# A transformer layer's gate-up projection: the next group's first split moved behind two result additions, and five raw buffers shared by all pairs

## The chip, the cores and the metric

The kernel runs on one core of one Trainium2 chip. The metric is the device time of one execution in microseconds (us). Before the change the median of 3 runs is 1850.49 us (1850.45 to 1850.53). Engines are named as the profile names them: PE is TensorE (matmul), PEld its weight loads, DVE is VectorE, ACT is ScalarE, POOL is GpSimd, SP is SyncE, whose queue issues most DMAs.

## The reference

One encoder layer on 256 tokens of width 2048, all in float32: a feed-forward half step, a mixer (a gated linear recurrence beside windowed attention), and a second feed-forward half step. The change lies in the feed-forward part, which the program runs twice:

```python
def swiglu(x, w_gate_up, w_down):
    gate, up = jnp.split(x @ w_gate_up, 2, axis=-1)
    return (jax.nn.silu(gate) * up) @ w_down

ff = swiglu(rms_norm(x, pre_norm_ffn1[layer]), w_ffn1_gate_up[layer], w_ffn1_down[layer])
x = x + 0.5 * rms_norm(ff, post_norm_ffn1[layer])
```

`x` is 256 x 2048, `w_gate_up` is 2048 x 11264 (5632 gate columns, then 5632 up columns), `w_down` is 5632 x 2048.

## The kernel before, in words

**Products.** Each float32 operand is held as two parts: h, the value rounded to the format that the PE multiplies in, and l, the remainder. A product of two operands takes three matmuls (h by h, h by l, l by h; `three`, lines 435 to 448). ACT makes h with a cast and DVE makes l with a subtraction (`split_act`, lines 175 to 177; L176 is every cast and L177 every such subtraction of the program). `split_half` does this for half of a raw tile, 128 x 1024, in h and l tiles of which there are five each.

**Groups and pairs.** The gate-up product is made in 11 groups g of 512 gate and 512 up columns. A group goes through the 2048 rows of the weight in 8 pairs u, each of two blocks of 128 rows. A pair's raw weights are one tile of 128 x 2048 floats, loaded in two DMAs of 512 KB. The result of a group stands in four banks of PSUM, `c[m][n]` with m the half of the tokens and n gate or up; below they are called c(m,n).

**Plain and mixed pairs.** A plain pair makes 8 products (24 matmuls). A mixed pair makes 7 (21 matmuls, `products`, lines 485 to 509), by the scheme that multiplies 2 x 2 blocks with seven products: some go to four further banks, p1, p5, p6 and p7, which have to be added to the c banks at the end of the group, and the weights have to be summed before they are split. In groups 2 to 10 pairs 2, 4, 5 and 6 are mixed, in group 1 pairs 2 and 4, in group 0 none (`MIXED_IN`, line 847). A mixed pair is prepared first (`prepare`, lines 894 to 906): its first block is split, and a DMA issued by POOL then adds its second block to the first in the raw tile. Its other three halves are split later (`splits`, lines 908 to 927).

**Loads before the change.** `plan` (lines 876 to 885) makes two lists, of the mixed and of the plain pairs. Mixed pairs use the pool `rawp` with three buffers, plain pairs the pool `room` with two. When the last half of a pair has been split, `load_next` takes the next pair of the same kind from its list and issues its two DMAs on SP (line 152, in `load`).

**Order of work.** From group 1 on the order of the instructions on each engine is the order in which the program states them (`tc.manual_schedule`, line 1167): splits are stated one pair ahead of the products that use them (`first_pairs`, `pair_ahead`). An engine takes its instructions in that order; semaphores alone hold it back.

**The boundary** (`boundary`, lines 1101 to 1127) ends each of the groups 1 to 9, so there are nine in each of the two feed-forward layers. Pair 7, the last one, is plain, and its products are stated bank by bank, c(0,0), c(1,0), c(0,1), c(1,1), six matmuls each (`bank`). Before each bank's products the mixed pairs' part is added to it on DVE:

- ACT copies p1 to a (L1112); c(0,0) += a (L1113)
- b = p6 + a (L1116); a = p7 + b (L1117); c(1,0) += a (L1118)
- b = p5 - b (L1121), formed in place; c(0,1) += b (L1122)
- b = p5 - a (L1124), formed in place; c(1,1) += b (L1125)

Between the first and the second of these lines stands the first half of the split of the next group's pair 0 (a cast on ACT and a subtraction on DVE); its second half stands behind the last. Pair 6, just ahead of the boundary, is mixed and writes last into p7, p6 and c(1,0), in this order. Behind the boundary `units` (lines 1033 to 1080) applies silu and the product of gate and up, and transposes the result.

Of the kernel before, what the change touches and what calls it, by code (L numbers as in the profile page):

```python
# [11 lines left out]
F32 = mybir.dt.float32  # L12
# [8 lines left out]
P = 128  # L21
# [3 lines left out]
KT = D // P  # L25
# [12 lines left out]
def hymba_layer_kernel(  # L38
# [25 lines left out]
    nc = tc.nc  # L64
# [3 lines left out]
    rawp = ctx.enter_context(tc.tile_pool(name="rawp", bufs=3))  # L68
# [7 lines left out]
    def nm(s):  # L76
        uid[0] += 1
        return f"{s}_{uid[0]}"
# [62 lines left out]
    def load(src, between=None, pool=rawp, **kw):  # L141
        raw = pool.tile([P, 2048], F32, tag="raw", name=nm("raw"), **kw)
        if len(src.shape) == 4:

            dst = raw.rearrange("p (a n b) -> p a n b", a=src.shape[1], n=src.shape[2])
            parts = [(dst[:, a], src[:, a]) for a in range(src.shape[1])]
        else:
            parts = [(raw.rearrange("p (a b) -> p a b", a=src.shape[1]), src)]
        for i, (to, of) in enumerate(parts):
            if i and between:  # L150
                between()
            nc.sync.dma_start(to, of)
        return raw
# [14 lines left out]
    def split_half(raw, i, hp=hip, lp=lop):  # L168
        part = raw[:, i * 1024 : (i + 1) * 1024]
        h = hp.tile([P, 1024], F32R, tag="h", name=nm("h"))  # L170
        l = lp.tile([P, 1024], F32R, tag="l", name=nm("l"))
        split_act(h, l, part)
        return h, l
# [24 lines left out]
    def close_far():  # L198
        far["cm"].__exit__(None, None, None)
# [193 lines left out]
    def sums_of(u, w):  # L393

        nc.vector.tensor_tensor(
            w[:, S3::2, :], u[:, 0, :].rearrange("p (m t) -> p m t", m=2), u[:, :, P:T], ALU.subtract
        )
        nc.vector.tensor_tensor(w[:, S2, :], w[:, S1, :], u[:, 0, 0:P], ALU.subtract)
        nc.vector.tensor_tensor(w[:, S4, :], u[:, 1, 0:P], w[:, S2, :], ALU.add)
        return w  # L400

    class Blocks:
# [4 lines left out]
        ahead = None  # L407
# [437 lines left out]
    LATE = 8  # L845

    MIXED_IN = (2, 4, 5, 6)
    AWAY = 8
    MIXED = range(0, 20, 2)
    MIXED_EARLY = MIXED[:8]  # L850
# [4 lines left out]
    class Gated(Blocks):  # L855
# [20 lines left out]
        def plan(self):  # L876

            self.here = {g: MIXED_IN if g > 1 else MIXED_IN[:2] for g in range(1, NG)}
            self.kinds = {True: [], False: []}
            for g in range(1, NG):  # L880
                for u in range(KT // 2):
                    self.kinds[u in self.here[g]].append((g, u))
            self.raws, self.firsts, self.split_of = {}, {}, {}
            for mixed in (False, True, False, True, True):
                self.load_next(mixed)

        def load_next(self, mixed):

            if self.kinds[mixed]:
                g, u = self.kinds[mixed].pop(0)  # L890
                kw = {} if mixed else {"pool": self.room, "bufs": 2}
                self.raws[g, u] = load(self.source(u, g), **kw)

        def prepare(self, g, u):

# [12 lines left out]
        def splits(self, g, u):  # L908

            raw = self.raws[g, u]  # L910
            got = self.split_of[g, u] = []
            if (g, u) in self.firsts:
                b11, b12, b21, b22 = (raw[:, i * 512 : (i + 1) * 512] for i in range(4))
                got.append(split_half(raw, 1))
                nc.vector.tensor_tensor(b22, b11, b22, ALU.add)
                nc.vector.tensor_tensor(b21, b22, b21, ALU.add)
                yield
                got.append(split_half(raw, 0))
                yield
                got.append(split_half(raw, 1))  # L920
                self.load_next(True)
            else:
                got.append(split_half(raw, 0))
                yield
                got.append(split_half(raw, 1))
                self.load_next(False)
            yield

        def take(self, g, u):
# [41 lines left out]
    def ffn(gated, w_dn, post_gain, again, gain=None, lead=None, aside=None):  # L971

        with ExitStack() as st:
            work = st.enter_context(tc.tile_pool(name=nm("wk"), bufs=1, reuse_waits="tile"))
            late = st.enter_context(tc.tile_pool(name=nm("hl"), bufs=LATE, reuse_waits="tile"))
            early_cm = tc.tile_pool(name=nm("he"), bufs=NU - LATE - AWAY, reuse_waits="tile")
            early = early_cm.__enter__()
# [5 lines left out]
            def room_for(tag):  # L983
                return work.tile([P, 512], F32, tag=tag, name=nm(tag))
# [21 lines left out]
            def even(u):  # L1006

                x = gated.tiles[u].rearrange("p k i t -> p (k i) t")
                nc.vector.tensor_tensor(
                    x, x.bitcast(F32), R[:, None, :].to_broadcast([P, 4, T]), ALU.mult  # L1010
                )

            def sums_in(u):
                x = gated.tiles[u].bitcast(F32)
                whole = room_for("z").rearrange("p (k t) -> p k t", k=2)
                nc.vector.tensor_tensor(whole, x[:, :, 0, :], x[:, :, 1, :], ALU.add)
                ws = sums_of(whole, room_for("s").rearrange("p (j t) -> p j t", j=4))
                apart = u == MIXED_IN[1]
                w = (gated.room if apart else work).tile(
                    [P, 4, 2, P], F32R, tag="sp", name=nm("xs"), bufs=1 if apart else 3  # L1020
                )
                split_act(w[:, :, 0, :], w[:, :, 1, :], ws)
                gated.sums[u] = w

            def put_away(u):
                away[u] = dram.tile([P, 1024], F32, tag=f"ht{u}", name=nm("away"))
                nc.sync.dma_start(away[u], hts[u].bitcast(F32).rearrange("p k i t -> p (k i t)"))
# [5 lines left out]
            def units(c, scale):  # L1033
# [34 lines left out]
                for bank in banks:  # L1068
                    g = len(hts)
                    u = bank.rearrange("p (k t) -> p k t", k=2)  # L1070
                    if g in MIXED_EARLY:
                        u = room_for("z").rearrange("p (k t) -> p k t", k=2)
                        nc.scalar.copy(u.rearrange("p k t -> p (k t)"), bank)
                    pool = early if AWAY <= g < NU - LATE else late
                    ht = pool.tile([P, 2, 2, T], F32R, tag="ht", name=nm("ht"))
# [6 lines left out]
            def some(steps, n):  # L1082
                for _ in range(n):
                    next(steps)
# [3 lines left out]
            for u in range(gated.pos, KT // 2):  # L1088
# [4 lines left out]
                for done in {4: (0, 1, 2), 5: (3, 4), 6: (5, 6), 7: (7,)}.get(u, ()):  # L1093
                    even(done)
                    if done in MIXED_IN[:2]:
                        sums_in(done)
# [4 lines left out]
            def boundary(g):  # L1101

                a, b = room_for("z"), room_for("s")
                c, (p1, p5, p6, p7) = gated.c, gated.p
                add = nc.vector.tensor_tensor
                rest_of = gated.take(g, last)

                def bank(m, n):
                    for k in range(2):
                        rest_of[4 * k + 2 * m + n]()  # L1110

                nc.scalar.copy(a, p1)  # L1112
                add(c[0][0], c[0][0], a, ALU.add)  # L1113
                ahead = gated.splits(g + 1, 0)
                next(ahead)
                add(b, p6, a, ALU.add)  # L1116
                add(a, p7, b, ALU.add)  # L1117
                add(c[1][0], c[1][0], a, ALU.add)  # L1118
                bank(0, 0)
                bank(1, 0)  # L1120
                add(b, p5, b, ALU.subtract)  # L1121
                add(c[0][1], c[0][1], b, ALU.add)  # L1122
                bank(0, 1)
                add(b, p5, a, ALU.subtract)  # L1124
                add(c[1][1], c[1][1], b, ALU.add)  # L1125
                bank(1, 1)
                next(ahead)

            def first_pairs(g, waiting):

                gated.group(g)
                some(waiting, 1)
                gated.prepare(g, MIXED_IN[1])
                some(waiting, 1)
                ahead = gated.splits(g, 1)
                some(ahead, 2)
                gated.prepare(g, MIXED_IN[2])
                for one in gated.take(g, 0):
# [9 lines left out]
            def pair_ahead(g, u):  # L1148

                ahead = gated.splits(g, u + 1)  # L1150
                next(ahead)
                if u + 1 == MIXED_IN[1]:
                    gated.prepare(g, MIXED_IN[3])
# [5 lines left out]
                if g == 1 and u in (4, 5):  # L1159
                    sums_in(MIXED_IN[u - 2])  # L1160
                if u == 5 and 1 < g <= AWAY // 2 + 1:
                    put_away(2 * g - 4)
# [4 lines left out]
            with tc.manual_schedule():  # L1167
                gated.prepare(1, MIXED_IN[0])
                some(gated.splits(1, 0), 2)
                for g in range(1, NG):  # L1170
# [3 lines left out]
                    if g < NG - 1:  # L1174
                        ahead = gated.splits(g, last)
# [24 lines left out]
            close_far()  # L1200
            back_cm = tc.tile_pool(name=nm("hb"), bufs=AWAY, reuse_waits="tile")
            back = back_cm.__enter__()
# [27 lines left out]
    def two_banks():  # L1230
        return [[pa(), pa()], [pb(), pb()]]

    gated = Gated(w_ffn1_gate_up[0], two_banks())
    xt = new_xt()
    gated.see(xt)
    with tc.manual_schedule():
# [9 lines left out]
        raw = rawp.tile([P, 2048], F32, tag="raw", name=nm("raw"))  # L1246
# [121 lines left out]
    with ExitStack() as s2:  # L1368
# [367 lines left out]
        for hp in range(4):  # L1736
            zf = headpair(2048 + hp * 256, "zf")
            if hp == 1:
                g = gates(0)
# [18 lines left out]
        g = gates(1)  # L1758
# [13 lines left out]
        gated = Gated(w_ffn2_gate_up[0], two_banks())  # L1772
# [80 lines left out]
```

## Time and profile before

| what | value |
|---|---|
| median of 3 runs | 1850.49 us |
| the profiled execution | 1851.23 us |
| its span, first to last instruction | 1849.5 us |
| PE busy | 1816.7 us, 98% |
| DVE busy | 1628.2 us, 88% |
| ACT busy | 1127.2 us, 61% |
| DMA | 422.42 MB, mean 228 GB/s |
| granted PE clock | 0.999 |

The span is cut in the profile into groups of instructions by line; a group's row gives busy time, the mean length of one and the idle time of the engine just ahead of them with what ended it. The chain of waits gives 53% of the span to L441, the line of all matmuls of `three`. Matmuls are pipelined: a 128x512 matmul is shown with 0.39 us, while the starts of two that follow each other without a stop are 0.23 us apart.

### The profile page before, as it was taken

To read this page: it belongs to the slowest core of one execution; us is meant where nothing else is said; L and a number is where in the kernel's file an instruction comes from. 1 tells how busy PE (TensorE), PEld (TensorE's weight loads), DVE (VectorE), ACT (ScalarE), POOL (GpSimd) and SP (SyncE) were. 2 spreads that over 40 slices of the span, in tenths; PEclk is the share of its full clock that TensorE was granted. 3 is DMA by queue.
4 is the path that set the end of the run, shared out by engine and by line. 5 is a ranking of instruction groups with operands and counts; after the bars stand their busy time and mean duration, and the time that the engine had idled before them with its cause. 6 is when DMAs were issued, how large, how long until landed. Compare 5 with 4: busy or idle time off the path is not lost.

```text
span 1849.5 us, 23264 instructions
## 1 busy us (share of the span) xinstructions
PE 1816.7 (98%) x8438; PEld 1504.2 (81%) x8438; DVE 1628.2 (88%) x2071; ACT 1127.2 (61%) x1492; POOL 114.3 (6%) x115
## 2 busy tenths in 40 slices
PE   9999999999999999999999999999999999999998
PEld 7877878888887888888888888878888778888886
DVE  7999999998999999477687788899999999999897
ACT  7565556655665557477587556555666556666563
POOL 1011111111000000000000000011111111000000
PEclk9999999999999999999999999999999999999999
DMA  8789999888756566656554456789999888865565
GB/s 298 228 219 275 274 268 256 247 244 251 272 186 226 196 248 211 208 175 181 166 171 148 169 212 245 220 237 262 272 272 254 255 246 237 262 236 206 183 237 183
DMA packets 200020, 422.42 MB, mean 228 GB/s; under 512 B 10984, under 2 KB 45888, under 8 KB 199136
## 3 DMA queue, kind: packets, MB, share of 16 engines
q1 hardware_dynamic: 178880, 380.95, 59.9%
q0 software_dynamic: 21024, 39.99, 12.9%
q8 instruction: 66, 1.08, 0.2%
q14 instruction: 50, 0.41, 0.1%
HBM read 408.29 MB, written 12.60 MB: 228 GB/s over the span
## 4 chain that ended last, share of the span: by engine, by line
PE 70%; DVE 14%; DMA 8%; ACT 4%; issue 3%; SPq 1%; POOL 0%; DVEq 0%; ACTq 0%; POOLq 0%
PE pa L441 28%; PE pb L441 25%; DVE l L177 8%; DMA raw<-in_w_ffn_gate_up_dram 6%; PE pa L309 5%; PE pa L314 3%; ACT h L176 3%; PE pa L364 2%; PE pa L363 2%; PE pa L362 2%; DMA raw<-in_w_ffn_down_dram 2%; DVE pb L1118 1%; DVE z L1117 1%; DVE pa L1113 1%; DVE s L1116 1%
## 5 line engine op out<-in xcount | busy, mean ns | idle before, releaser
L176 ACT CAST h<-raw 128x1024 fp32r<-128x1024 f32 (+1 forms) x861 | 846.7, 1013 | 454.2 <-PE pb L441 113.2
L177 DVE TENSOR_TENSOR l<-raw,h 128x1024 fp32r<-128x1024 f32 (+1 forms) x861 | 985.0, 1170 | 136.8 <-ACT h L176 105.5
L441 PE MATMUL pa<-h,xt 128*128 128x512 f32 x1104 | 387.5, 392 | 0.2
L441 PE MATMUL pb<-h,xt 128*128 128x512 f32 x952 | 341.1, 393 | 17.5 <-DVE pb L1118 17.5
L441 PEld LDWEIGHTS pa<-h,xt 128*128 128x128 f32 x1104 | 207.4, 188 | 44.3 <-DVE xt L232 0.6
L441 PEld LDWEIGHTS pb<-h,xt 128*128 128x128 f32 x952 | 178.6, 188 | 64.4 <-DVE pb L1118 25.1
L441 PE MATMUL pa<-l,xt 128*128 128x512 f32 x552 | 215.7, 391 | 0.0
L441 PE MATMUL pb<-l,xt 128*128 128x512 f32 x476 | 185.5, 390 | 0.0
L441 PE MATMUL pb<-h,ht 128*128 128x512 f32 x464 | 163.5, 390 | 0.0
L441 PE MATMUL pa<-h,ht 128*128 128x512 f32 x464 | 162.7, 389 | 0.0
L901 POOL DMA_DIRECT2D raw<-in_w_ffn_gate_up_dram x76 | 92.0, 1211 | 758.1 <-DVE l L177 709.1
L309 PE MATMUL pa<-xt,h 128*128 128x512 f32 x512 | 124.4, 392 | 0.2 <-ACT h L176 0.2
L441 PEld LDWEIGHTS pa<-l,xt 128*128 128x128 f32 x552 | 103.9, 188 | 20.6 <-DVE l L177 0.7
L309 PEld LDWEIGHTS pa<-xt,h 128*128 128x128 f32 x512 | 93.8, 188 | 18.6 <-ACT h L176 0.6
L441 PE MATMUL pa<-h,xs 128*128 128x512 f32 x304 | 105.9, 389 | 0.0
L441 PE MATMUL pb<-h,xs 128*128 128x512 f32 x304 | 105.9, 389 | 0.0
L441 PEld LDWEIGHTS pb<-l,xt 128*128 128x128 f32 x476 | 89.4, 188 | 17.1
L441 PEld LDWEIGHTS pa<-h,ht 128*128 128x128 f32 x464 | 87.1, 188 | 18.2
L441 PEld LDWEIGHTS pb<-h,ht 128*128 128x128 f32 x464 | 87.1, 188 | 18.1
L441 PE MATMUL pb<-l,ht 128*128 128x512 f32 x232 | 90.3, 389 | 0.0
L441 PE MATMUL pa<-l,ht 128*128 128x512 f32 x232 | 90.3, 389 | 0.0
L314 PE MATMUL pa<-xt,l 128*128 128x256 f32 x512 | 69.1, 285 | 0.0
(289 smaller groups left out, 2517.6 us busy)
## 6 DMA issues: line engine op xcount, KB each, us to landing
raw<-in_w_ffn_gate_up_dram SPq DMA_DIRECT2D x350, 512.0 KB, 5.3
raw<-in_w_ffn_down_dram SPq DMA_DIRECT2D x88, 1024.0 KB, 5.2
raw<-in_w_mix_in_dram SPq DMA_DIRECT2D x52, 1024.0 KB, 5.0
raw<-in_w_ffn_gate_up_dram POOLq DMA_DIRECT2D x76, 512.0 KB, 8.3
raw<-in_w_mix_out_dram SPq DMA_DIRECT2D x16, 1024.0 KB, 5.0
away<-ht SPq DMA_DIRECT2D x16, 512.0 KB, 6.6
ht<-away SPq DMA_DIRECT2D x16, 512.0 KB, 7.4
pg<-in_post_norm_ffn_dram SPq DMA_DIRECT2D x4, 512.0 KB, 6.8
```

Source lines behind the costliest of these rows:

```text
L176: nc.scalar.copy(hi, src)
L177: nc.vector.tensor_tensor(lo, src, hi.bitcast(F32), ALU.subtract)
L309: nc.tensor.matmul(slot[f], weights(hs, kk, f), xcol(xt, k), start=(k == 0), stop=(k == KT - 1))
L314: nc.tensor.matmul(slot[f][:, 0:T], weights(ls, kk, f), xcol(xt, kh * 8 + kk, 0), start=False, stop=False,)
L362: nc.tensor.matmul(dst, xh, h[:, o : o + n], start=(k == 0), stop=False)
L363: nc.tensor.matmul(dst, xh, l[:, o : o + n], start=False, stop=False)
L364: nc.tensor.matmul(dst, xl, h[:, o : o + n], start=False, stop=(k == KT - 1))
L441: nc.tensor.matmul(self.bank(at), lhs, rhs, start=(n == 1), stop=n in (ends, self.of[at]), skip_group_check=n > ends,)
L901: nc.gpsimd.dma_start(raw[:, 0:1024].rearrange("p (k c) -> p k c", k=2), self.source(u, g)[:, :, 1], accum_op=ALU.add,)
L1113: add(c[0][0], c[0][0], a, ALU.add)
L1116: add(b, p6, a, ALU.add)
L1117: add(a, p7, b, ALU.add)
```

## The change

In `boundary` the two lines that begin the split of the next group's pair 0 move from behind the first result addition to behind the products of bank c(0,1), that is, past the additions into c(1,0) and c(0,1). All pairs are put into one list, sorted by the place at which the first use of the pair is stated: for a plain pair its own number, for a mixed pair the place of its `prepare` (`PREPARED`). The five raw buffers, three in `rawp` and two in `room`, are made once and shared; the pair whose split has ended gives its buffer to the next one on the list.

```diff
     MIXED_IN = (2, 4, 5, 6)
+    PREPARED = {2: -0.5, 4: 0.5, 5: 1.5, 6: 3.5}
...
             self.here = {g: MIXED_IN if g > 1 else MIXED_IN[:2] for g in range(1, NG)}
-            self.kinds = {True: [], False: []}
+            wanted = []
             for g in range(1, NG):
                 for u in range(KT // 2):
-                    self.kinds[u in self.here[g]].append((g, u))
+                    before = PREPARED[u] if u in self.here[g] else u
+                    wanted.append((g * KT // 2 + before, g, u))
+            self.wanted = [at[1:] for at in sorted(wanted)]
             self.raws, self.firsts, self.split_of = {}, {}, {}
-            for mixed in (False, True, False, True, True):
-                self.load_next(mixed)
-
-        def load_next(self, mixed):
-
-            if self.kinds[mixed]:
-                g, u = self.kinds[mixed].pop(0)
-                kw = {} if mixed else {"pool": self.room, "bufs": 2}
-                self.raws[g, u] = load(self.source(u, g), **kw)
+            for pool, n in ((rawp, 3), (self.room, 2)):
+                for _ in range(n):
+                    raw = pool.tile([P, 2048], F32, tag="raw", name=nm("raw"), bufs=n)
+                    self.load_next(raw)
+
+        def load_next(self, raw):
+
+            if self.wanted:
+                g, u = self.wanted.pop(0)
+                dst = raw.rearrange("p (k n c) -> p k n c", k=2, n=2)
+                for k in range(2):
+                    nc.sync.dma_start(dst[:, k], self.source(u, g)[:, k])
+                self.raws[g, u] = raw
...
                 got.append(split_half(raw, 1))
-                self.load_next(True)
+                self.load_next(raw)
             else:
                 got.append(split_half(raw, 0))
                 yield
                 got.append(split_half(raw, 1))
-                self.load_next(False)
+                self.load_next(raw)
...
                 nc.scalar.copy(a, p1)
                 add(c[0][0], c[0][0], a, ALU.add)
-                ahead = gated.splits(g + 1, 0)
-                next(ahead)
                 add(b, p6, a, ALU.add)
                 add(a, p7, b, ALU.add)
                 add(c[1][0], c[1][0], a, ALU.add)
...
                 add(b, p5, b, ALU.subtract)
                 add(c[0][1], c[0][1], b, ALU.add)
                 bank(0, 1)
+                ahead = gated.splits(g + 1, 0)
+                next(ahead)
                 add(b, p5, a, ALU.subtract)
                 add(c[1][1], c[1][1], b, ALU.add)
                 bank(1, 1)
```

With the pairs of a group from 2 to 9 written by their number, and those of the next group with a dash, the loads behind the ends of splits 0 to 7 were those of 3, 7, 6, 0', 2', 4', 5', 1' before and are 3, 6, 7, 2', 0', 4', 1', 5' now.

## Prediction

> **What bounds the kernel now.** I read the page first, for the share of each engine; then the groups and the waits, for what stops TensorE; then the timeline of one boundary between two gate-up groups, engine by engine. The page and its groups:
>
> ```profile
> span 1849.5 us, 23264 instructions
> PE 1816.7 (98%) x8438; PEld 1504.2 (81%) x8438; DVE 1628.2 (88%) x2071; ACT 1127.2 (61%) x1492; POOL 114.3 (6%) x115
> ...
> L441 PE MATMUL pb<-h,xt 128*128 128x512 f32 x952 | 341.1, 393 | 17.5 <-DVE pb L1118 17.5
> ```
>
> The waits, in which a row gives the total, the number and the longest in us:
>
> ```profile
> ACT h L176 <- DMA raw<-in_w_ffn_gate_up_dram: 64.6, 41, 4.2
> ...
> PEld pb L441 <- DVE pb L1118: 25.1, 18, 2.0
> ...
> PE pb L441 <- DVE pb L1118: 17.5, 18, 1.6
> ...
> PEld pb L441 <- DVE pb L1125: 3.1, 18, 0.2
> ```
>
> TensorE (PE) is busy for 98% of the span, so only its stops can be won back, and the largest is in the lines that change: 18 waits for L1118, the addition into bank c(1,0). There are 18 because each of the two feed-forward layers has nine boundaries. ScalarE (ACT) waits 41 times for a gate-up load, but no row has TensorE waiting for one. How full VectorE (DVE) is over one whole group, from one boundary's first product to the next one's:
>
> ```profile
> 1306.36:1349.21 42.85, 42.02 (x190) 34.46 (x188) 39.88 (x48) 26.06 (x30) 4.84 (x5) 1.00 0.93 269
> ```
>
> The columns are the length, then busy time of PE, PEld, DVE, ACT and POOL, the granted clock, the DMA share and GB/s. DVE works 39.88 of 42.85 us, nearly as much as TensorE: a boundary is a race between two full engines.
>
> That boundary on TensorE, by start and duration (three products of 128x512 make one pass, six the part of a bank):
>
> ```profile
> 1304.78 0.62 PE L441 MATMUL pb<-h,xs 128*128 128x512 f32 x2
> ...
> 1305.45 0.39 PE L441 MATMUL pb<-h,xs 128*128 128x512 f32 x1
> ...
> 1306.36 0.39 PE L441 MATMUL pa<-h,xt 128*128 128x512 f32 x1
> ...
> 1308.71 0.50 PE L441 MATMUL pb<-h,xt 128*128 128x512 f32 x1 [0.82 <-DVE pb L1118]
> ...
> 1310.22 0.39 PE L441 MATMUL pa<-h,xt 128*128 128x512 f32 x1
> ...
> 1311.60 0.39 PE L441 MATMUL pb<-h,xt 128*128 128x512 f32 x1
> ...
> 1312.95 0.39 PE L441 MATMUL pa<-h,xt 128*128 128x512 f32 x1
> ```
>
> 1305.45 is the last product into p6 (end 1305.84). The rest of pair 7 starts at 1306.36 with c(0,0), then c(1,0) at 1308.71, c(0,1) at 1310.22, c(1,1) at 1311.60; the next group's pair 0 starts at 1312.95. Six products without a stop take 1.36 (1312.95 - 1311.60 = 1.35, 1311.60 - 1310.22 = 1.38), the six after a stop 1.51, so a restart costs about 0.14 beside the wait. Without a wait c(1,0) would start at 1307.72; it starts 0.99 later. The same stretch on VectorE:
>
> ```profile
> 1304.71 0.69 DVE L1113 TENSOR_TENSOR pa<-pa,z 128x512 f32<-128x512 f32 x1
> 1305.31 1.21 DVE L177 TENSOR_TENSOR l<-raw,h 128x1024 fp32r<-128x1024 f32 x1
> 1306.44 0.68 DVE L1116 TENSOR_TENSOR s<-pb,z 128x512 f32<-128x512 f32 x1
> 1307.16 0.69 DVE L1117 TENSOR_TENSOR z<-pb,s 128x512 f32<-128x512 f32 x1
> 1307.95 0.70 DVE L1118 TENSOR_TENSOR pb<-pb,z 128x512 f32<-128x512 f32 x1
> 1308.56 0.68 DVE L1121 TENSOR_TENSOR s<-pa,s 128x512 f32<-128x512 f32 x1
> 1309.28 0.70 DVE L1122 TENSOR_TENSOR pa<-pa,s 128x512 f32<-128x512 f32 x1
> 1310.01 0.69 DVE L1124 TENSOR_TENSOR s<-pa,z 128x512 f32<-128x512 f32 x1
> 1310.73 0.70 DVE L1125 TENSOR_TENSOR pb<-pb,s 128x512 f32<-128x512 f32 x1
> ```
>
> The queue has no hole: c(0,0)'s addition, the split's subtraction l that the change moves, then p6, p7 and c(1,0), which ends at 1308.65, 0.06 before TensorE goes on. The reader is to see the last row too: c(1,1)'s addition ends at 1311.43, only 0.17 before TensorE starts on that bank, and a wait of 0.2 of the weight load stands on it in the list of waits.
>
> **Part 1: the split moved behind c(1,0) and c(0,1).** Its cast on ACT has no other ACT instruction to pass, and stays. Its subtraction moves on DVE from before p6 to after c(0,1); what is behind it there is p5's last subtraction and c(1,1)'s addition, for which TensorE waits. It issues no DMA itself, and passes none on SP or POOL. All DVE work ahead of c(1,1) is the same set of instructions in another order, so c(1,1) can't be ready earlier than now unless DVE idled, and at this boundary it doesn't.
>
> It can be ready later. p6's addition, which now starts at 1306.44, is free to follow c(0,0) at 1305.31, but it reads p6, written until 1305.84. How soon an engine starts behind a product is in this row, whose product is the first of the two at 1304.78 (end 1305.17):
>
> ```profile
> 1305.20 1.06 ACT L176 CAST h<-raw 128x1024 fp32r<-128x1024 f32 x1 [0.26 <-PE pb L441]
> ```
>
> 0.03 after the end; I take 0.04 for DVE, so p6 starts at 1305.88, and DVE idles about half a us where it never idled. From there, with start-to-start steps of the rows above: p7 +0.72, c(1,0) +0.79 and 0.70 long, end 1308.09, TensorE starts on c(1,0) at 1308.15 (now 1308.71). That stop shrinks by 0.56 and stays at 0.43. p5 at +0.61 after c(1,0)'s start (1308.00), c(0,1) at +0.72, end 1309.42; TensorE comes to c(0,1) at 1308.15 + 1.51 = 1309.66 without a wait. Then the moved subtraction: +0.60 after c(0,1)'s start (as 1304.71 to 1305.31), 1309.32; p5 again +1.13 (1305.31 to 1306.44), 1310.45; c(1,1) +0.72, 1311.17 to 1311.87; TensorE 1311.93. It would have been there at 1309.66 + 1.38 = 1311.04: a new stop of 0.89, with a second restart. The next group starts at 1311.93 + 1.36 + 0.14 = 1313.43 instead of 1312.95: **0.47 to 0.48 us later.** I take 0.47.
>
> The unknown in this is p6's start. The earliest, with no wait for the product, is 1305.31: then c(1,1) ends at 1311.30, 0.13 earlier than now, TensorE is 0.24 earlier there and pays 0.14 for the stop, and the boundary gains 0.1. The program's order excludes that end, since the addition must read a finished bank. The latest is what a later end of the matmuls than the modelled one would give; 0.1 there is 0.1 on each boundary. I stand at 1305.88, by the nearest row.
>
> Five of the 18 boundaries are not like this one:
>
> ```profile
> 97.66 0.50 PE L441 MATMUL pb<-h,xt 128*128 128x512 f32 x1 [1.34 <-DVE pb L1118]
> 184.58 0.51 PE L441 MATMUL pb<-h,xt 128*128 128x512 f32 x1 [1.59 <-DVE pb L1118]
> 270.65 0.50 PE L441 MATMUL pb<-h,xt 128*128 128x512 f32 x1 [1.14 <-DVE pb L1118]
> 1222.93 0.50 PE L441 MATMUL pb<-h,xt 128*128 128x512 f32 x1 [1.34 <-DVE pb L1118]
> 1437.86 0.50 PE L441 MATMUL pb<-h,xt 128*128 128x512 f32 x1 [1.38 <-DVE pb L1118]
> ```
>
> The other 13 must average (17.5 - 6.8) / 13 = 0.82, the case above. In these five DVE comes late, by 0.52, 0.77, 0.32, 0.52 and 0.56, together 2.69 us. After the change the first 0.57 of a delay (1305.31 to 1305.88) only fill the new idle time, so those boundaries end where the others do; at most 0.2 of the 0.77 is left. So 18 x 0.47 = 8.5, less 2.7 for the five: **+5.8 us.**
>
> **Part 2: five raw buffers, in order of need.** The loads are the same number and size; each split end still frees one buffer and issues one load behind it on SP, which only carries another pair. In groups 2 to 10 pairs 1, 2 and 6 come one split earlier, pairs 0, 5 and 7 one later. What this can win:
>
> ```profile
> 1313.76 1.05 ACT L176 CAST h<-raw 128x1024 fp32r<-128x1024 f32 x1 [1.04 <-DMA raw<-in_w_ffn_gate_up_dram]
> ...
> 1329.98 3.53 ACT L176 CAST h<-raw 128x512 fp32r<-128x512 f32 x4 [1.96 <-DMA raw<-in_w_ffn_gate_up_dram]
> ```
>
> These are the casts of pair 1 and of pair 6, both waiting for a load that is now issued earlier. But ACT is busy 26.06 us of 42.85, and behind both casts TensorE runs on without a stop until the next boundary. In the worst group DVE waits behind such a cast:
>
> ```profile
> 1404.15 1.23 DVE L177 TENSOR_TENSOR l<-raw,h 128x1024 fp32r<-128x1024 f32 x1 [2.81 <-ACT h L176]
> ```
>
> and the late boundary at 1437.86 follows it. So the load order mends lateness that Part 1 already counts as absorbed: 0 more. Pair 5, now last, is needed some 10 us after its issue, behind pair 1's casts: 0.
>
> The Trainium skill (Perfetto Trace Analysis, § Optimization Strategy) says that a gap which repeats on the engine that should be full can mean that buffers for the next tile ran out. By that rule Part 2 would end the stop; here all 18 stops name an addition and none a load, so the sum keeps 0 for it, and the rule's case is a rival.
>
> At the first group of layer 1, pair 0 takes the place in SP's order that pair 4 had, behind the bias table. Pair 4's cast waited there until 54.99, and pair 0's subtraction and first product stand close behind:
>
> ```profile
> 54.99 0.62 ACT L176 CAST h<-raw 128x512 fp32r<-128x512 f32 x1 [4.19 <-DMA raw<-in_w_ffn_gate_up_dram]
> ```
> ```profile
> 55.65 1.22 DVE L177 TENSOR_TENSOR l<-raw,h 128x1024 fp32r<-128x1024 f32 x1
> ```
> ```profile
> 57.19 0.39 PE L441 MATMUL pa<-h,xt 128*128 128x512 f32 x1
> ```
>
> The cast (1.05) now ends at 56.04, the subtraction some 57.3, and the product that needs it runs at 57.42: it just fits, with later ones 0.1 or 0.2 short. Between 0 and 1 us, once; I take 0.2. In layer 2 pair 0 is issued behind pair 6's split instead, long before its use: 0.
>
> **Sum.** +5.8 + 0 + 0.2 = +6.0 us. The profiled execution took 1851.23 (span 1849.5 and 1.7 around it), the median is 1850.49; the difference stands on either, and the median gives **1856.5 us**.
>
> **Rivals.**
> 1. *Forecast: the stop moves from c(1,0) to c(1,1)*, 1854.3 to 1858.5. For it: the 0.17 between L1125 and TensorE, and p6's end. Chance 0.66.
> 2. *DVE takes p6 earlier than 1305.88, or fills the gap.* Then the gain at c(1,0) and the loss at c(1,1) nearly cancel: from -0.1 to +0.2 a boundary, less part of the 2.7: 1848 to 1854. Against it: the order gives DVE nothing to fill the gap with. Chance 0.16.
> 3. *The stop is a matter of buffers, and ends* (the other side). It decides where DVE reaches c(0,0) early because its casts no longer wait for loads, by a whole 1.1 us, so that c(1,1) too is ready before TensorE. Price: at most the 0.99 + 0.14 of the 13 and the five with 2.69 more, 18 x 1.13 + 2.7 = 23 us, 1827; half of it 1839. Against it: p6 is TensorE's own product, so c(1,0) is never ready before 1308.09 whatever DVE does. Chance 0.10.
> 4. *The new load order makes waits of its own*, pair 5 or pair 0 landing late in groups with DMA at 0.93. One wait as long as the longest now, 4.2, in each of two groups, less the slack of about 3 us that DVE has in a group: 1 to 3 us more, 1858.5 to 1862. Chance 0.08.
> That the change doesn't do what it says is no rival: in the built order the subtraction stands behind c(0,1).
>
> **The numbers.** A measurement can tell about 0.2% (3.7 us) from no change. Rival 1 and 4 are slower by more than that, 0.74, less 0.03 for the low edge; rival 2 is within it, with that edge 0.19; rival 3 is faster. So faster 0.1, same 0.19, slower 0.71. Rivals 1 and 2 hold 0.82; the range 1850 to 1860 takes all of 1, most of 2 and half of 4, some 0.8. The likeliest case alone has 1854.3 to 1858.5.
>
> **What would show it.** In the waits of the changed kernel: the 18 for c(1,0) fall from 0.82 to about 0.3 each; 18 new ones for c(1,1)'s addition of about 0.7 to 0.9; p6's addition has an idle time before it that a product ends; the period of a group goes from 42.85 to about 43.3; ACT's waits for gate-up loads fall well under 64.6. If c(1,1)'s waits are missing, Part 1 is wrong; if the period is under 42.5, rival 3 holds; if PE waits for a cast or a load within a group, rival 4.

## The result, and the profile after

The changed kernel takes 1859.11 us (1857.9 to 1860.48; before in the same measurement 1850.49, 1850.28 to 1851.46): a ratio of 1.0046 (1.0032 to 1.0061), 8.6 us slower. A second measurement of the same kernel on another chip gave 1858.5 against 1850.78, 1.0035 (1.0022 to 1.0047), 7.7 us slower. The profiled execution of the changed kernel took 1858.14, with a span of 1856.4: 6.9 above that of before.

First the page of the changed kernel. TensorE is shown busy 4.6 us longer, part of it because the first product behind a stop is shown with 0.50 and not 0.39; the idle time in front of the products into `pb` names another line than before:

```profile
span 1856.4 us, 23305 instructions
...
PE 1821.3 (98%) x8438; PEld 1502.6 (81%) x8438; DVE 1628.7 (88%) x2071; ACT 1127.4 (61%) x1492; POOL 114.4 (6%) x115
...
L441 PE MATMUL pb<-h,xt 128*128 128x512 f32 x952 | 342.8, 395 | 18.3 <-DVE pb L1132 13.5
```

In the changed kernel L1120 is c(0,0)'s addition, L1121 p6's, L1122 p7's, L1123 c(1,0)'s, L1126 and L1127 those for c(0,1), L1131 p5's last subtraction and L1132 c(1,1)'s addition. Its waits (total, number, longest):

```profile
PEld pb L441 <- DVE pb L1132: 21.2, 18, 1.3
...
ACT h L176 <- DMA raw<-in_w_ffn_gate_up_dram: 20.5, 15, 5.0
...
PE pb L441 <- DVE pb L1132: 13.5, 18, 0.8
PEld pb L441 <- DVE pb L1123: 12.4, 18, 0.7
...
DVE s L1121 <- PE pb L441: 7.7, 16, 0.5
...
PE pb L441 <- DVE pb L1123: 4.8, 18, 0.3
```

There are now two stops at each of the 18 boundaries instead of one: 13.5 / 18 = 0.75 at c(1,1), and 4.8 / 18 = 0.27 at c(1,0). The fifth row is new too: VectorE itself waits for a product, p6's, 16 times; in group 1 pair 6 is plain and p6 has long been written, so the other two of the 18 don't have this wait. ScalarE's waits for gate-up loads fell from 64.6 to 20.5. A whole group, from one boundary's first product to the next one's:

```profile
1310.14:1353.47 43.33, 42.32 (x189) 34.45 (x188) 39.90 (x48) 25.97 (x30) 4.83 (x5) 1.00 0.91 267
```

The group takes 43.33 where it took 42.85, with VectorE's work unchanged (39.90 against 39.88). The boundary that answers to the one shown of before, on VectorE:

```profile
1308.49 0.69 DVE L1120 TENSOR_TENSOR pa<-pa,z 128x512 f32<-128x512 f32 x1
1309.66 0.69 DVE L1121 TENSOR_TENSOR s<-pb,z 128x512 f32<-128x512 f32 x1 [0.48 <-PE pb L441]
1310.39 0.69 DVE L1122 TENSOR_TENSOR z<-pb,s 128x512 f32<-128x512 f32 x1
1311.19 0.70 DVE L1123 TENSOR_TENSOR pb<-pb,z 128x512 f32<-128x512 f32 x1
1311.80 0.68 DVE L1126 TENSOR_TENSOR s<-pa,s 128x512 f32<-128x512 f32 x1
1312.51 0.70 DVE L1127 TENSOR_TENSOR pa<-pa,s 128x512 f32<-128x512 f32 x1
1313.12 1.22 DVE L177 TENSOR_TENSOR l<-raw,h 128x1024 fp32r<-128x1024 f32 x1
1314.25 0.69 DVE L1131 TENSOR_TENSOR s<-pa,z 128x512 f32<-128x512 f32 x1
1314.97 0.70 DVE L1132 TENSOR_TENSOR pb<-pb,s 128x512 f32<-128x512 f32 x1
```

and on TensorE:

```profile
1310.14 0.39 PE L441 MATMUL pa<-h,xt 128*128 128x512 f32 x1
...
1311.94 0.50 PE L441 MATMUL pb<-h,xt 128*128 128x512 f32 x1 [0.27 <-DVE pb L1123]
...
1315.72 0.50 PE L441 MATMUL pb<-h,xt 128*128 128x512 f32 x1 [0.73 <-DVE pb L1132]
...
1317.23 0.39 PE L441 MATMUL pa<-h,xt 128*128 128x512 f32 x1
```

The reader is to see the exchange. VectorE's hole is in front of p6's addition; the split's subtraction (1313.12) now stands between c(0,1) and c(1,1); TensorE starts on c(1,0) 0.55 earlier than before (1.80 behind c(0,0)'s first product, 2.35 before) and on c(1,1) 0.34 later (5.58, 5.24 before), so the new stop costs it more than it had won. The six products behind the second stop take 1.51 (1317.23 - 1315.72), so a second restart of about 0.14 is paid as well. The next group starts at 7.09 here, where it started at 6.59.

All boundary times below are counted so, from the first product into c(0,0). For each kernel, the medians over groups 2 to 9 of both layers, read from the timelines:

| kernel | p6's addition starts | c(1,0) ready | c(1,1) ready | next group starts | period |
|---|---|---|---|---|---|
| before | 0.08 | 2.29 | 5.07 | 6.62 | 42.87 |
| after | -0.48 | 1.74 | 5.52 | 7.08 | 43.35 |
| split_only | -0.48 | 1.74 | 5.52 | 7.08 | 43.35 |
| loads_only | 0.08 | 2.29 | 5.07 | 6.60 | 42.85 |
| behind_four | -0.48 | 1.74 | 4.52 | 6.05 | 42.30 |
| after_p6_early | -1.06 | 1.15 | 4.93 | 6.48 | 42.74 |
| both_halves | -0.48 | 1.74 | 6.66 | 8.21 | 44.46 |
| before_p6_early | 0.39 | 2.60 | 5.38 | 6.93 | 43.20 |
| before_p6_p7 | 0.08 | 2.36 | 5.14 | 6.69 | 42.94 |
| four_p6_early | -1.06 | 1.15 | 3.94 | 5.49 | 41.75 |
| four_p6_p7 | -1.06 | 1.22 | 4.00 | 5.55 | 41.81 |

### The profile page after: what moved, and what is told of

Read it like the earlier page. It is cut to its first block, busy times and chain, and to the rows that moved or that the text cites. A ratio compares the mean times of both kernels' runs of the same rounds, so it can differ in the third digit from the quotient of the medians.

```text
span 1856.4 us, 23305 instructions
## 1 busy us (share of the span) xinstructions
PE 1821.3 (98%) x8438; PEld 1502.6 (81%) x8438; DVE 1628.7 (88%) x2071; ACT 1127.4 (61%) x1492; POOL 114.4 (6%) x115
## 4 chain that ended last, share of the span: by engine, by line
PE 79%; DVE 13%; ACT 3%; issue 2%; DMA 2%; SPq 0%; POOL 0%; DVEq 0%; ACTq 0%; POOLq 0%
PE pa L441 33%; PE pb L441 29%; DVE l L177 5%; PE pa L309 5%; PE pa L314 3%; PE pa L364 2%; PE pa L362 2%; PE pa L363 2%; DMA raw<-in_w_ffn_down_dram 2%; ACT h L176 1%; DVE pb L1132 1%; DVE z L1122 1%; DVE pb L1123 1%; DVE raw L473 1%; DVE s L1121 1%
## 5 line engine op out<-in xcount | busy, mean ns | idle before, releaser
L441 PE MATMUL pb<-h,xt 128*128 128x512 f32 x952 | 342.8, 395 | 18.3 <-DVE pb L1132 13.5
L1046 ACT ACTIVATE z<-pa,scales 128x512 f32<-128x512 f32 x22 | 15.1, 687 | 91.0 <-PE pa L441 89.9
```

Of the source, the lines that this page charges most:

```text
L441: nc.tensor.matmul(self.bank(at), lhs, rhs, start=(n == 1), stop=n in (ends, self.of[at]), skip_group_check=n > ends,)
```

## The experiments

**Theory A**, that of the forecast: the stop is the place of c(1,0)'s and c(1,1)'s additions in VectorE's order, and p6's addition can't start before p6's last product. **Theory B**: the stop is a matter of raw buffers and loads, or the load order is what costs. Times are medians; each ratio is to the kernel before on the same chip.

### Each half of the change alone

*split_only*, the kernel before with nothing but the moved lines:

```diff
                 add(c[0][0], c[0][0], a, ALU.add)
-                ahead = gated.splits(g + 1, 0)
-                next(ahead)
...
                 bank(0, 1)
+                ahead = gated.splits(g + 1, 0)
+                next(ahead)
```

> The split moved as in the change, the loads as before. Theory A (the stop moves from bank c(1,0) to bank c(1,1), because DVE waits for p6's last product and then has the split ahead of c(1,1)'s addition): each boundary's next group starts 7.07 us after the boundary's first product, as in the changed kernel, instead of 6.6; two or three late boundaries stay up to 0.2 us later; 1856 to 1858 us. Theory B (the new load order brings the loss): like the kernel before or faster, 1850 us or less.

Measured 1856.73, ratio 1.0033 (1.0021 to 1.0045). Its waits:

```profile
ACT h L176 <- DMA raw<-in_w_ffn_gate_up_dram: 56.2, 40, 4.3
...
PE pb L441 <- DVE pb L1125: 13.4, 18, 0.8
...
PE pb L441 <- DVE pb L1116: 4.8, 18, 0.3
```

L1125 is c(1,1)'s addition here, L1116 c(1,0)'s: the same two stops of the same length as in the whole change, while the loads wait nearly as before.

*loads_only*, the changed kernel with the two lines back behind c(0,0)'s addition (the diff above, read the other way):

> The shared buffers and the load order of the change, the split where it was before. Theory A: the stop stays at c(1,0) with 0.82 us in all groups of four mixed pairs; the three boundaries that came late behind a load (0.77, 0.32, 0.56 us) become like the others, the first group costs 0.2 more: 1849 us, between 1848 and 1850. Theory B: some 6 to 8 us slower than before, 1857 to 1859.

Measured 1851.44, ratio 1.0003 (0.9994 to 1.0012). Its waits:

```profile
PEld pb L441 <- DVE pb L1125: 23.5, 18, 1.8
...
ACT h L176 <- DMA raw<-in_w_ffn_gate_up_dram: 19.9, 16, 5.3
...
PE pb L441 <- DVE pb L1125: 15.9, 18, 1.3
```

L1125 is c(1,0)'s addition here. ScalarE's waits for gate-up loads fall from 64.6 us to 19.9, and the 18 stops stay, with 15.9 in place of 17.5: three boundaries that a load had made late are now regular, worth 1.6 us of stops in the profile (span 1848.1 against 1849.5), which the times can't tell from nothing. Theory A expected 1.5 less than before and at most 1850; the time is 1.4 above that, so the size isn't confirmed. Theory B is out for the stop.

### The split behind all four additions

*behind_four*:

```diff
                 bank(0, 1)
-                ahead = gated.splits(g + 1, 0)
-                next(ahead)
                 add(b, p5, a, ALU.subtract)
                 add(c[1][1], c[1][1], b, ALU.add)
                 bank(1, 1)
+                ahead = gated.splits(g + 1, 0)
+                next(ahead)
```

> As the changed kernel, but the split stands behind all four additions. Theory A: c(1,1)'s addition ends 1.13 us earlier, 4.4 us after the boundary's first product, before TensorE comes there at 4.66; the stop at c(1,0) stays at 0.43; the next group starts at 6.02 to 6.05 instead of 7.07: 18 x 1.03 = 18.5 us less than the changed kernel, 1840 to 1841, 10 less than before. Theory B (the wait for c(1,1) has another cause than the split in front of it): 1856 to 1859.

Measured 1840.27, ratio 0.9942 (0.993 to 0.9954). c(1,1) is ready at 4.52, 1.00 earlier than in the changed kernel (1.13 was expected), and the stop there is gone: L1130, its addition here, holds only weight loads. The stop at c(1,0) is left as it was:

```profile
PE pb L441 <- DVE pb L1123: 4.8, 18, 0.3
...
PEld pb L441 <- DVE pb L1130: 3.2, 18, 0.2
```

So the place of one subtraction of 1.13 us against c(1,1)'s addition decides whether the change costs 8 us or wins 10.

*both_halves* goes the other way, with both halves of the split ahead of c(1,1):

```diff
                 ahead = gated.splits(g + 1, 0)
                 next(ahead)
+                next(ahead)
                 add(b, p5, a, ALU.subtract)
                 add(c[1][1], c[1][1], b, ALU.add)
                 bank(1, 1)
-                next(ahead)
```

> The changed kernel, with the second half of pair 0's split put ahead of c(1,1)'s addition as well. Theory A: one more subtraction of 1.13 us stands ahead of c(1,1) on VectorE, which has no idle time there, so c(1,1)'s addition ends at 6.65 in place of 5.52 and each of the 18 boundaries is 1.13 later: 20.3 us over the changed kernel, 1877 to 1881. Rival (VectorE's place in the boundary isn't what sets TensorE's stop at c(1,1)): as the changed kernel, 1857 to 1860.

Measured 1882.64, ratio 1.0176 (1.0162 to 1.0189).

```profile
PE pb L441 <- DVE pb L1133: 34.0, 18, 1.9
```

L1133 is c(1,1)'s addition here. c(1,1) is ready at 6.66 and the next group starts at 8.21, as expected to 0.02; 34.0 - 13.5 = 20.5 more waiting. The time is 1.6 above the expected range, because the first boundary of each layer, behind the group with two mixed pairs, loses 2.7 and not 1.1 (its period is 46.05 against 43.32). The rest of that loss is no wait on VectorE. TensorE at the first of them, and the row of the 3.41 us from 102.72 on:

```profile
101.71 0.50 PE L441 MATMUL pb<-h,xt 128*128 128x512 f32 x1 [1.92 <-DVE pb L1133]
...
103.17 0.63 PE L441 MATMUL pb<-h,xt 128*128 128x512 f32 x1
103.60 0.63 PE L441 MATMUL pa<-h,xt 128*128 128x512 f32 x1
```
```profile
102.72:106.13 3.41, 3.41 (x9) 2.63 (x8) 2.98 (x4) 3.41 (x5) 1.21 (x1) 0.50 0.45 154
```

The granted clock, the third figure from the end, is 0.50 there, and matmuls start 0.43 apart instead of 0.23; eight of them cost 8 x 0.20 = 1.6, and 1.13 + 1.6 = 2.7. Layer 2's first boundary shows the same behind a stop of 1.94. Behind the other 16 stops, of 1.87 to 1.90, the clock stays at 1.00; what decides it is not shown.

### p6's product earlier

What holds p6's addition is p6's product, by theory A. In the last mixed pair, pair 6, the product into c(0,1) is put behind the one into p6, which then ends 0.68 earlier:

```diff
-            for at, left, right in (
+            steps = [
...
-            ):
+            ]
+            if isinstance(self, Gated) and u == MIXED_IN[3]:
+                steps.insert(5, steps.pop(2))
+            for at, left, right in steps:
```

This edit was put on three kernels. *four_p6_early* is behind_four with it:

> As behind_four, and in the last mixed pair the product into c(0,1) is made behind the one into p6, so that p6 is done 0.68 us earlier. Theory A: p6's addition follows c(0,0)'s without a hole, c(1,0) is ready before TensorE comes there, and neither stop is left in groups 2 to 9: the next group starts 5.45 to 5.5 after the boundary's first product; 16 boundaries at 1.6 and two (group 1) at 1.05 under the changed kernel: 28 us less, 1829 to 1833. Rival C: DVE, 39.9 us busy in a group of then 41.8, becomes the bound; its additions come later than 1.0 before the first product and part of the stop stays: 1834 to 1841.

Measured 1831.0, ratio 0.9889 (0.9876 to 0.9902): the fastest version of all. VectorE and TensorE at one boundary:

```profile
1291.38 0.69 DVE L1123 TENSOR_TENSOR pa<-pa,z 128x512 f32<-128x512 f32 x1
1291.98 0.68 DVE L1124 TENSOR_TENSOR s<-pb,z 128x512 f32<-128x512 f32 x1
...
1296.27 0.70 DVE L1133 TENSOR_TENSOR pb<-pb,s 128x512 f32<-128x512 f32 x1
```
```profile
1293.04 0.39 PE L441 MATMUL pa<-h,xt 128*128 128x512 f32 x1
...
1294.39 0.39 PE L441 MATMUL pb<-h,xt 128*128 128x512 f32 x1
...
1298.52 0.39 PE L441 MATMUL pa<-h,xt 128*128 128x512 f32 x1
```

p6's addition (L1124) follows c(0,0)'s without a hole, and TensorE passes the boundary with no stop: 5.48 for the 24 matmuls, where the changed kernel needs 7.08.

*after_p6_early* is the changed kernel with it:

> The changed kernel, with one edit: in the last mixed pair of a group the product into p6 is made one place earlier, ahead of the one into c(0,1), in the 16 boundaries of groups 2 to 9. Theory A (the order of additions on VectorE, held at the start of p6's addition by p6's own last product): p6's addition starts about 0.57 us earlier (-1.05 relative to c(0,0)'s first product in place of -0.48), TensorE no longer stops at c(1,0), the stop at c(1,1) stays near 0.9 less what the earlier start leaves, and the next group starts at about 6.5 in place of 7.07: 16 x 0.57 = 9.1 under the changed kernel, 1849 to 1851. Rival (the product isn't what holds p6's addition, or the stop is a matter of buffers): as the changed kernel, 1857 to 1860.

Measured 1848.1, ratio 0.999 (0.9981 to 0.9999). p6's addition at -1.06, the next group at 6.48: 16 x 0.60 = 9.6 under the changed kernel's boundaries, and the time 0.9 under the expected range. The stop at c(1,1) is still there (12.7 us in 18), so the changed order loses on that bank even when VectorE has no hole.

*before_p6_early* is the kernel before with it:

> The kernel before, with p6's product made one place earlier in the last mixed pair, as in the other kernel with that edit. Theory A: with the split's subtraction still ahead of it, p6's addition starts at 0.08 by VectorE's own queue and not by the product, so nothing changes: 1849.5 to 1851.5, 18 stops of 0.8 at c(1,0). Rival (the earlier product by itself is worth something, by the order of TensorE's work): 9 us less, 1840 to 1843.

Measured 1857.05, ratio 1.0036 (1.0023 to 1.0048): slower, which neither theory had. ScalarE and VectorE at one boundary (first product into c(0,0) at 1351.27), and below them ScalarE's cast in the kernel before:

```profile
1349.43 1.05 ACT L176 CAST h<-raw 128x1024 fp32r<-128x1024 f32 x1 [0.62 <-PE pb L441]
```
```profile
1349.61 0.69 DVE L1116 TENSOR_TENSOR pa<-pa,z 128x512 f32<-128x512 f32 x1
1350.51 1.23 DVE L177 TENSOR_TENSOR l<-raw,h 128x1024 fp32r<-128x1024 f32 x1 [0.21 <-ACT h L176]
```
```profile
1303.88 1.05 ACT L176 CAST h<-raw 128x1024 fp32r<-128x1024 f32 x1
```

The cast of the next pair 0 starts 1.84 ahead of that product; before it was 2.48 (1303.88 against 1306.36), and no wait stood in front of it. The product into c(0,1) is the last one to read a pair of h and l tiles, of which there are five each. Moved, it holds its h tile 2 us longer; the cast waits until p7's product, the one into `pb` that the row names, has freed another (that product ends 1.88 ahead, the cast starts 0.04 later). The subtraction waits for the cast, and stands ahead of p6's addition: 0.39 instead of 0.08, and 0.33 more in each period. In the two kernels above the split is stated behind p6's addition, which a late cast can't hold up; p6's addition starts at -1.06 in both.

*before_p6_p7* tests that: p6's product earlier by a change of place with p7's, c(0,1)'s product left where it was.

```diff
-                steps.insert(5, steps.pop(2))
+                steps.insert(4, steps.pop(5))
```

> The kernel before, with p6's product made ahead of p7's in the last mixed pair, and the product into c(0,1) left in its place. Theory A': the 0.3 us a boundary that the kernel before lost with p6's product ahead of c(0,1)'s came from the tile that c(0,1)'s product reads: it stayed in use 2.0 us longer, the first cast of the next split waited for it or for its neighbour (0.62, a product named) and the split stood 0.3 later in front of p6's addition. With that product in its place the cast starts as before (2.48 ahead of c(0,0)'s first product), p6's addition starts at 0.08, and nothing changes: 1849.5 to 1851.5. Rival (an earlier p6 costs by itself, by what it moves on TensorE or in the profile): 1855 to 1858 again.

Measured 1851.74, ratio 1.0004 (0.9995 to 1.0013): the cast starts 2.48 ahead, p6's addition at 0.08, and the loss is gone. *four_p6_p7* is the fastest kernel with this edit in place of the other:

> The changed kernel with the split behind all four additions and p6's product ahead of p7's, the product into c(0,1) in its place. Theory A: p6's product ends at the same point as in the fastest kernel so far (2.05 ahead of c(0,0)'s first product begins), p7 one product later than there but still 0.4 ahead of its addition, so the boundaries are the same, next group at 5.5: 1829 to 1832. Rival (what made the fastest kernel fast was the later product into c(0,1), not the earlier p6): 1839 to 1841, as with the split behind four additions alone.

Measured 1832.03, ratio 0.9893 (0.9879 to 0.9906): what pays is p6's earlier end, by either edit.

### What the shared buffers are worth

*four_p6_old_loads* is four_p6_early with the loads of the kernel before; the diff is the load part of the change, taken back:

```diff
-        def load_next(self, raw):
+        def load_next(self, mixed):
...
-            if self.wanted:
-                g, u = self.wanted.pop(0)
+            if self.kinds[mixed]:
+                g, u = self.kinds[mixed].pop(0)
```

> The fastest kernel so far (split behind all four additions, p6's product earlier: 1831.0) with the loads as they were before: five buffers by kind of pair. Theory A: the load order only brings VectorE to some boundaries late, by 0.77, 0.32 and 0.56 in three of them; c(1,0)'s addition is now ready 0.2 before TensorE needs it, so up to 0.57, 0.12 and 0.36 of that, about 1 us, shows: 1831 to 1833. Rival (with the stops gone the loads set the pace, so the shared buffers are what the faster order needs): 1836 or more.

Measured 1839.69, ratio 0.9944 (0.993 to 0.9957): 8.7 above four_p6_early, or 9.4 when each is counted from the kernel before on its own chip. Theory A's size for the loads, about 1 us, was wrong here, and the rival's 1836 or more came true. One group of four_p6_old_loads, ScalarE and VectorE:

```profile
1308.82 3.47 ACT L176 CAST h<-raw 128x1024 fp32r<-128x1024 f32 x4 [3.08 <-DMA raw<-in_w_ffn_gate_up_dram]
```
```profile
1309.90 2.96 DVE L177 TENSOR_TENSOR l<-raw,h 128x1024 fp32r<-128x1024 f32 x3 [2.31 <-ACT h L176]
...
1324.55 3.50 DVE L177 TENSOR_TENSOR l<-raw,h 128x1024 fp32r<-128x1024 f32 x3 [0.26 <-ACT h L176]
```

and the same group of four_p6_early, VectorE's waits and the row of the group:

```profile
1313.62 1.23 DVE L177 TENSOR_TENSOR l<-raw,h 128x1024 fp32r<-128x1024 f32 x1 [0.28 <-ACT h L176]
...
1323.87 2.59 DVE L177 TENSOR_TENSOR l<-raw,h 128x1024 fp32r<-128x1024 f32 x2 [0.81 <-ACT h L176]
```
```profile
1293.04:1334.80 41.76, 41.76 (x190) 34.53 (x189) 39.84 (x48) 26.31 (x31) 4.87 (x5) 1.00 0.94 277
```

In a group of 41.76 VectorE has 41.76 - 39.84 = 1.92 to spare. With the old loads it waits 2.31 + 0.26 = 2.57 behind casts that wait for a load, and comes late to the boundary; with the shared buffers 1.09. Eight boundaries of four_p6_old_loads start their next group at 6.13 to 6.40 instead of 5.49, together 6.3. TensorE also stops ahead of c(0,0) in two of them (0.28 and 0.22) and once in the middle of a group for a subtraction (0.57 at 244.02), each with a restart. From the first boundary to the ninth the two profiles differ by 4.4 in layer 1 and 3.7 in layer 2, together 8.2; the spans differ by 7.6. In a period of 42.87, where there are 3 us to spare, the same loads cost nothing that the times show (loads_only).

### Does the load part cost anything in the changed kernel?

The whole change came out 2.6 above the forecast and split_only 0.2 above it. Both were run again, on one chip; *split_again* is split_only, *after_again* the changed kernel, without further edit.

> The split moved, the loads as before, a second time beside the whole change. Theory A (the loads are worth nothing once the split has moved): within 1.5 us of the whole change, both 1856 to 1859. Rival (the shared buffers cost some us of their own beside the moved split, which would be the 2.6 by which the whole change came out above my forecast): 2 us or more below the whole change.

> The whole change a second time, on the chip of the run with the split alone. Theory A: boundaries as in its first profile (c(1,1)'s addition ends at 5.52, the next group at 7.07), the time within 1.5 us of the split alone, 1856 to 1859. Rival (the loads add a cost of their own): 2 us or more above it, with waits or a longer period within the groups that the split alone does not have.

Measured 1857.32 (1.0028, 1.0017 to 1.0039) and 1858.5 (1.0035, 1.0022 to 1.0047): 1.2 apart, with intervals that overlap and the same boundaries in both profiles (5.52 and 7.07). From the first boundary to the end of the ninth both take 353.7 to 353.8 in each layer, so the load part costs nothing there. From the start of layer 1's last group to layer 2's first boundary, where no order of additions is touched, the eight kernels with shared buffers take 773.9 to 776.5 (mean 774.9) and the six with the old ones 773.5 to 775.1 (mean 774.0). Two of the eight, behind_four and four_p6_p7, ran 3.4 us of this stretch (from 565.3 and from 1179.3) at a granted clock of 0.50, some 1.5 us lost in each; without that the means are 0.5 apart. That may hold a cost of about half a us, or none; it stays open.

## Why the prediction was right or wrong

**Part 1, the mechanism and its size: right.** Worked out for the boundary shown: p6's addition 0.48 ahead of c(0,0)'s first product, c(1,0) ready at 1.73, c(1,1) at 5.51, the next group at 7.07. Measured -0.48, 1.74, 5.52, 7.08. The estimate of 0.04 from a product's end to VectorE's start, taken from ScalarE's 0.03, held. All the steps after it were start-to-start distances from rows of the same instructions in the profile of before, and these did not change with the order. The stops came out at 0.27 and 0.75, where I had said about 0.3 and 0.7 to 0.9.

**The five late boundaries: right.** All 18 are alike after the change (7.07 to 7.09), and in split_only too, where the loads still come late: its boundary near 268 begins late, and the wait in front of p6's addition is 0.23 instead of 0.48. The hole takes up the delay. In the profiles, from the first boundary to the end of the ninth, layer 1 grew by 2.18 and layer 2 by 3.19, together 5.4 for the 5.8 worked out. Some 0.2 of the missing 0.4 is lateness that I had read too low: the boundary at 181.33 also stopped TensorE ahead of c(0,0), and the period before it was 43.10 where regular ones took 42.87.

**Part 2, the loads at 0: right for this change.** In the changed order, after_again and split_again can't be told apart; in the old order loads_only is at 1.0003, and ScalarE's waits fell by two thirds without a gain that the times show. But the reason given, that the new order only mends lateness which the hole absorbs, holds only as long as VectorE has room: with both stops gone the same loads are worth 8.7 us.

**The entry, 0.2: about right.** Pair 0's cast took the place that I had put it in, and the weight loads behind it waited for its two subtractions, by the 0.1 or 0.2 that I had read:

```profile
55.00 1.05 ACT L176 CAST h<-raw 128x1024 fp32r<-128x1024 f32 x1 [5.03 <-DMA raw<-in_w_ffn_gate_up_dram]
```
```profile
57.36 0.19 PEld L441 LDWEIGHTS pa<-l,xt 128*128 128x128 f32 x1 [0.20 <-DVE l L177]
...
60.23 0.19 PEld L441 LDWEIGHTS pa<-l,xt 128*128 128x128 f32 x1 [0.26 <-DVE l L177]
```

TensorE has no idle time there in this profile, but two matmuls start 0.05 and 0.11 late. All eight kernels with shared buffers have one or both of these waits, and none of the six with the old loads has one there; the starts of the matmuls there lose between 0 and 0.55, 0.2 on average (after_again, with 0.55, has a stop of 0.17 among it). The time of the first boundary alone, 95.04 against 94.80, couldn't show this: it is 94.80 to 95.16 with the old loads and 95.00 to 95.59 with the shared buffers.

**The sum, +6.0 against 7.7 and 8.6: too low.** The first measurement lies 0.6 above the likeliest case's range and inside the wide one, the second at the likeliest case's upper edge. The two measurements of split_only are 5.9 and 6.5 above the kernel before on their chips, which is the forecast; the whole change is higher, with intervals that overlap. The boundaries give 5.4 of 6.9 in the profile. Of the rest, 0.95 lies between layer 1's last group and layer 2's first boundary, 0.34 behind layer 2's last and 0.24 at the entry. No step of mine had a term for the first two, and the kernels scatter there by more (773.5 to 776.5 and 277.9 to 280.2).

**The rivals.** Rival 2 (p6 earlier, or the gap filled) needs VectorE to pass p6's product; the product held it 16 times of 16, and only an earlier product moved it. Rival 3 (a matter of buffers) is out by loads_only. The Trainium skill (Perfetto Trace Analysis, § Optimization Strategy) says that a gap that repeats can mean that buffers for the next tile ran out. Here the gap repeated 18 times and new buffers left it, 15.9 us of 17.5, while the order of instructions removed it. Rival 3's price wasn't far off, though: with no stop in groups 2 to 9 and the loads in order the kernel takes 1831, by another way than that rival's. Rival 4 (waits of the new load order's own) did not happen beyond the entry: no wait of TensorE in the changed kernel names a gate-up load.

## What to carry to other kernels

In a queue that is taken in order, moving work behind a consumer pays only if it is moved behind every consumer that is short of time: here the last one got the delay, and the hole that opened in front was lost as well. Count what the engine at the front will wait for next (here its own partner's product), and move that too. A better load order that is worth nothing beside another bound should be tried again when that bound is gone: here it went from 0 to 8.7 us.

## What the runs showed of the hardware that was not expected

*A second engine to wait for cost 0.07 us on VectorE.* With p7's product behind p6's, p7's addition waits for VectorE's own result and for TensorE. In before_p6_p7 a semaphore instruction stands in front of it in the 16 boundaries with a mixed pair 6:

```profile
L1120 DVE TENSOR_TENSOR z<-pb,s x18: 691/692/692, 96.3 to 1566.4; 128x512 f32<-128x512 f32 x18
L1120 DVEq EVENT_SEMAPHORE  x16: 21/21/21, 139.2 to 1566.3; - x16
```
```profile
1307.53 0.68 DVE L1119 TENSOR_TENSOR s<-pb,z 128x512 f32<-128x512 f32 x1
1308.31 0.69 DVE L1120 TENSOR_TENSOR z<-pb,s 128x512 f32<-128x512 f32 x1
```

The instruction is shown with 21 ns, but p7's addition starts 0.10 behind p6's end and not 0.04 as before (1308.31 against 1308.21; 1307.16 against 1307.12), although the product had ended 1.4 us earlier. c(1,0) is ready at 2.36 instead of 2.29, and the period is 42.94 instead of 42.87. four_p6_p7 has 41.81 where four_p6_early has 41.75; that this is the same 0.07 is likely and not shown.

*Who reads a tile last can matter as much as who writes first.* In before_p6_early a product that was moved by 2 us on TensorE delayed none of the matmuls next to it, and cost 0.33 a group by way of a free tile, a cast and a subtraction on two other engines.

*The granted clock fell behind a few stops.* It was 0.50 for 3.4 us behind the stops of 1.92 and 1.94 in both_halves, and once each in behind_four (behind stops of 0.78 and 0.75 near 564) and four_p6_p7 (behind 0.84 and 0.93 near 1177). Behind 16 stops of 1.87 to 1.90 in both_halves it was 1.00, so the length of the stop alone doesn't decide it.
